# Output projection requests the attention's rows from its fifth chunk on, at its third chunk

## The chip, the cores and the metric

The kernel runs on one core of a Trainium2 chip. The metric is the device time of the program in microseconds (us), the median of several runs.

## The reference

One decoder block on 1024 tokens of width 1024, in f32. A joint projection `h @ w_in` feeds two groups of heads: an mLSTM (512 columns of output) and causal softmax attention with low-rank queries and keys (512 columns). Both outputs stand side by side and one output projection maps them back; then come a cross-attention into 256 memory tokens and a squared-ReLU MLP of hidden width 4096.

```python
y_m = jax.nn.sigmoid(o_pre) * hm.reshape(Bn, S, M_WIDTH)       # mLSTM group, 512 wide
...
o_a = causal_block_attention(q_full, k_full, v_a.transpose(0, 2, 1, 3))
y_a = rmsnorm(o_a.transpose(0, 2, 1, 3), a_out_g).reshape(Bn, S, A_WIDTH)
return jnp.concatenate([y_m, y_a], axis=-1) @ w_out
...
x = x + parallel_mixer(h, ...)
x = x + memory_cross_attention(rmsnorm(x, norm_x_g[l]), mem_n, ...)
x = x + jnp.square(jax.nn.relu(rmsnorm(x, norm_ffn_g[l]) @ w_ff1[l])) @ w_ff2[l]
```

So the first 512 of the 1024 inner columns of the product with `w_out` come from the mLSTM, the last 512 from the attention.

## The kernel before, in words

Every large product is cut into chunks of 128 inner columns. A chunk holds 12 matmuls of 128x512: 4 blocks of 128 outputs, each in three passes over high and low parts of the operands (`PASSES`). The parts are made by `split`: a cast on ACT (the high part) and a subtraction on DVE (the low part, the tiles `wu` and `yT`). Four PSUM banks with the tag `g` hold a group's sums.

The order of the work around the change comes from two things. `products(groups)` (L242) is a generator that walks the chunks of a list of groups: at each chunk it issues loads up to `ahead` = 3 chunks further on, splits one chunk further on, and then emits 4 blocks of matmuls, with `yield 0.65` after each. `Weaver.weave` (L152) takes these as fill: for each it lets attention tasks run for a share of its cost set by the group's `ratio`, chosen by priority and by modelled clocks. When the generator yields a list of names instead, `weave` calls `until`, which runs tasks and no fill at all until all those named are done. The order so written is then arranged again for each engine when the program is built; on the chip each engine takes its instructions in its own order.

The groups are, one after the other, the input projection of both token halves, the memory's keys and values, the output projection `w_out(0)` of tokens 0 to 511 (two groups of 512 outputs, 8 chunks each) and the query projection of the cross-attention for the same half (`q_group`, matmuls `g<-wu,x1s`). The attention tasks run beside `w_out(0)` and `q_group`: for each of 8 blocks of 128 queries two `mla_kv` (tiles `pk`, `ka`, `kT`), two `mla_q` (`pq`, `qa`, `rt`, `t`, `qT`), four `attn` (scores `pAS`, exponentials `P`, their transposes `pPT` copied to `PT`, sums `po`) and one `attn_fin` (L1080), which scales the rows `ya` by `as` (made on GpSimd) and writes them to `yd` in HBM (L1096). `w_out(1)`, for tokens 512 to 1023, comes when all attention tasks are done.

`w_out(h)` (L1099) reads back its rows from `yd`: chunk k loads `yr` (L1108) for four query blocks, from the mLSTM's half of `yd` for k = 0 to 3 and from the attention's half for k = 4 to 7. Four transposes (`pyT`), a cast and a subtraction make `yT`. Its first group names `need` = fin0 to fin3 (h = 0) or fin4 to fin7 (h = 1). In `products` this need does two things: loads ahead stop at the group's first chunk as long as one of those tasks is open, and at chunk 0 the list is yielded.

After the last attention task the program copies the query projection's sums to `xq` on DVE and ACT (with squares, `jkv` on DVE and `jk` on ACT, straight from the banks `g`), reads eight tiles `res` back, and transposes `xq` (`pxq`).

Of the kernel before, what the change touches and what calls it, by code (L numbers as in the profile page):

```python
# [19 lines left out]
NK = 8  # L20
# [15 lines left out]
class Engine:  # L36


    def __init__(self, eng, log, fixed, per):
        self.eng, self.log, self.fixed, self.per = eng, log, fixed, per  # L40
# [132 lines left out]
class Group:  # L173


    def __init__(self, w, c0, cols, act, evac, fm, nk=NK, gain=None, nblk=4, need=None, mkact=None, res=None, mark=None, pre=None, ratio=None):
        self.w, self.c0, self.cols, self.act, self.evac, self.fm = w, c0, cols, act, evac, fm
        self.nk, self.gain, self.nblk, self.need, self.mkact, self.res, self.mark, self.pre, self.ratio = (
            nk, gain, nblk, need, mkact, res, mark, pre, ratio)


class Trunk:
# [59 lines left out]
    def products(self, groups):  # L242

        T, ahead, near = self.T, self.ahead, self.near
        steps = [(g, k) for g in groups for k in range(g.nk)]
        loaded, units, ready = {}, {}, {}
        banks = [0.0] * 4
        nl = ns = 0
        ps = None
        for n, (g, k) in enumerate(steps):  # L250
            while nl < len(steps) and nl <= n + ahead:
                gg, kk = steps[nl]
                if gg.mkact is not None:
                    if gg.need is not None and nl > n:
                        if any(x not in self.wv.done for x in gg.need):
                            break
                    gg.mkact(kk, True)
                raw = self.raw([P, gg.cols])
                self.S.dma_start(raw, gg.w[kk * P:(kk + 1) * P, gg.c0:gg.c0 + gg.cols])
                loaded[nl] = raw  # L260
                nl += 1
            while ns < nl and ns <= n + near:
                gg, kk = steps[ns]
                if gg.mkact is not None:
                    gg.mkact(kk, False)
                u = self.wu([P, 2, gg.cols])
                self.split(u[:, 0], u[:, 1], loaded.pop(ns), None if gg.gain is None else self.vec(gg.gain, kk))
                ready[ns] = self.wv.settle(0.0)
                units[ns] = u
                ns += 1  # L270
            if k == 0:
                if g.mark is not None:
                    yield g.mark
                if g.ratio is not None:
                    yield (g.ratio,)
                if g.pre is not None:
                    yield from g.pre()
                if g.need is not None:
                    yield g.need
                ps = [self.pg.tile([P, HT], F32, tag="g", name="g") for _ in range(g.nblk)]  # L280
            u = units.pop(n)
            for j in range(g.nblk):
                for i, (x, y) in enumerate(PASSES):
                    st, sp = (k == 0 and i == 0), (k == g.nk - 1 and i == 2)
                    if g.fm:
                        T.matmul(ps[j], lhsT=u[:, x, j * P:(j + 1) * P], rhs=g.act[k][:, y, :], start=st, stop=sp)
                    else:
                        T.matmul(ps[j][:, :g.cols], lhsT=g.act[k][:, x, j * P:(j + 1) * P], rhs=u[:, y, :],
                                 start=st, stop=sp)
                self.wv.fready = 0.0  # L290
                if j == g.nblk - 1:
                    self.wv.fready = ready.get(n + 1, 0.0)
                elif k == 0:
                    self.wv.fready = banks[j + 1]
                yield 0.65
            if k == g.nk - 1:
                for j in range(g.nblk):
                    if g.res:
                        yield g.res
                    self.wv.settle(0.0)  # L300
                    g.evac(j, ps[j])
                    banks[j] = self.wv.settle(0.0)
                yield 0.0
# [141 lines left out]
    ratio = (1.416, 1.465, 1.465, 1.465, 1.465, 0.678, 1.0, 1.0, 0.5, 0.5, 1.186, 0.61, 0.915)  # L445
# [653 lines left out]
    def w_out(self, h):  # L1099

        V, S, T = self.V, self.S, self.T
        act, loc = [None] * NK, {}
        res = h == 1

        def mkact(k, load):
            if load:
                loc[k] = self.raw([P, 4, P], "yr")
                S.dma_start(loc[k], self.yd[4 * h:4 * h + 4, k // 4, :, (k % 4) * P:(k % 4 + 1) * P]  # L1108
                            .rearrange("b p d -> p b d"))
                return  # L1110
            ps = self.mp(name="pyT")
            for j in range(4):
                T.transpose(ps[:, j * P:(j + 1) * P], loc[k][:, j, :], self.ident)
            t = self.ap.tile([P, 2, HT], F32R, tag="act", name="yT")
            self.split(t[:, 0], t[:, 1], ps)
            act[k] = t

        def evac(g):
            def ev(j, ps):
                k = 4 * g + j  # L1120
                if k == 0:
                    loc["st"] = self.scr.tile([P, HT], F32, tag="st", name="st1", bufs=1)
                xr = self.raw([P, HT], "xres")
                S.dma_start(xr, self.a["xT"][k * P:(k + 1) * P, h * HT:(h + 1) * HT])
                if not res:
                    V.tensor_tensor(xr, ps, xr, ALU.add)
                    S.dma_start(self.x1d[k], xr)
                    self.stats_add(loc["st"], xr, k == 0)
                else:
                    V.tensor_tensor(self.R[h][k], ps, xr, ALU.add)  # L1130
                    self.stats_add(loc["st"], self.R[h][k], k == 0)
                if k == NK - 1:
                    self.stats_cols(loc["st"], self.v1[h], None)
            return ev

        need = [f"fin{4 * h + j}" for j in range(4)]
        w = self.a["w_out"]
        return [Group(w, 0, 512, act, evac(0), True, gain="gy", need=need, mkact=mkact),
                Group(w, 512, 512, act, evac(1), True, gain="gy")]


# [645 lines left out]
```

## Time and profile before

| what | value |
|---|---|
| runs | 1261.75, 1263.88, 1268.05 us; median 1263.88 |
| the profiled execution | 1264.9 us, span 1263.1 us |
| mean granted clock | 0.997 |
| PE busy | 1234.6 us, 98% of the span |
| DVE busy | 894.9 us, 71% |
| ACT busy | 662.0 us, 52% |
| GpSimd busy | 72.6 us, 6% |

Read it so: PE is what the kernel is made of, and 1 us less idle time on PE is at most 1 us less of the whole. The stretches that matter here are the attention's, from about 263 us to 464 us, and the passage to the cross-attention behind it, up to about 490 us. A row of a timeline gives the start, the duration, the engine, the line, the operation with its output and inputs, the number of alike instructions in a row, and in brackets the idle time before it with what ended it. Nearly all rows carry L56, the helper that records every operation, so the tile names are what to go by.

### The profile page before, as it was taken

How to read it: one execution, taken by the hardware profiler on the slowest of the kernel's cores; microseconds unless marked ns; L12 is line 12 of the kernel's file. 1: busy time of each engine (PE TensorE's matmuls, PEld its weight loads, DVE VectorE, ACT ScalarE, POOL GpSimd, SP SyncE). 2: the span in 40 equal slices, each digit the busy share in tenths (PEclk: the TensorE clock that was granted, in tenths of full speed). 3: DMA queues.
4: the chain of work that ended last, by engine and by line, in shares of the span. 5: the costliest groups of instructions: out<-in, count | busy, mean ns of one | idle time of the engine just before them, and what ended most of it. 6: DMA issues, size and time to landing. Idle time of an engine off the chain costs nothing.

```text
span 1263.1 us, 17573 instructions
## 1 busy us (share of the span) xinstructions
PE 1234.6 (98%) x6030; PEld 1011.2 (80%) x6030; DVE 894.9 (71%) x1919; ACT 662.0 (52%) x1536; POOL 72.6 (6%) x90
## 2 busy tenths in 40 slices
PE   7999999999999999999999999999999999999998
PEld 5777777777888887888777888888888888888887
DVE  5886897898757556757889976567657959654653
ACT  6466645688645446636655444454444444444442
POOL 1100100143200001001000000000000000000000
PEclk9999999999999999999999999999999999999999
DMA  7345533312124255332434654534399943333431
GB/s 242 89 117 176 161 99 109 117 60 92 51 92 126 87 179 178 99 126 100 167 101 133 210 190 167 184 136 147 117 334 314 319 149 101 100 100 100 155 129 66
DMA packets 113168, 180.65 MB, mean 143 GB/s; under 512 B 8472, under 2 KB 40120, under 8 KB 113080
## 3 DMA queue, kind: packets, MB, share of 16 engines
q1 hardware_dynamic: 113080, 179.55, 43.1%
q8 instruction: 47, 0.77, 0.3%
q14 instruction: 41, 0.34, 0.1%
HBM read 134.41 MB, written 45.11 MB: 142 GB/s over the span
## 4 chain that ended last, share of the span: by engine, by line
PE 81%; DVE 7%; DMA 4%; issue 4%; ACT 3%; POOL 1%; SPq 0%; POOLq 0%; DVEq 0%; ACTq 0%
PE gf L56 46%; PE g L56 21%; PE pAS L56 3%; PE po L56 2%; DMA xr<-in_xT_dram 1%; PE pPT L56 1%; DVE res L56 1%; PE pxo L56 1%; DMA xt<-in_x_dram 1%; DVE wu L56 1%; PE pq L56 1%; ACT wu L56 1%; PE pyT L56 1%; PE pxS L56 1%; PE qkps L56 1%
## 5 line engine op out<-in xcount | busy, mean ns | idle before, releaser
L56 PE MATMUL gf<-hu,w2u 128*128 128x512 f32 x1344 | 304.8, 389 | 0.0
L56 PEld LDWEIGHTS gf<-hu,w2u 128*128 128x128 f32 x1344 | 252.3, 188 | 52.4
L56 PE MATMUL gf<-xT,w1u 128*128 128x512 f32 x768 | 183.2, 397 | 2.1 <-ACT w1u L56 2.1
L56 PEld LDWEIGHTS gf<-xT,w1u 128*128 128x128 f32 x768 | 145.0, 189 | 37.9 <-ACT w1u L56 2.8
L56 ACT CAST hu<-hr 128x512 fp32r<-128x512 f32 x112 | 69.8, 624 | 169.7 <-PE gf L56 169.7
L56 PE MATMUL g<-wu,xs 128*128 128x512 f32 (+1 forms) x576 | 143.2, 399 | 10.1 <-ACT wu L56 7.5
L56 DVE TENSOR_TENSOR hu<-hr,hu 128x512 fp32r<-128x512 f32 x112 | 77.2, 689 | 100.9 <-ACT hu L56 100.9
L56 PEld LDWEIGHTS g<-wu,xs 128*128 128x128 f32 x576 | 106.6, 190 | 37.5 <-ACT wu L56 9.0
L56 PE MATMUL gf<-xB,w1u 128*128 128x512 f32 x576 | 135.1, 392 | 0.0
L56 PEld LDWEIGHTS gf<-xB,w1u 128*128 128x128 f32 x576 | 108.0, 188 | 24.4 <-issue 0.5
L56 ACT CAST w1u<-w1r 128x512 fp32r<-128x512 f32 x96 | 58.9, 619 | 116.1 <-PE gf L56 114.5
L56 DVE TENSOR_TENSOR wu<-raw,wu 128x512 fp32r<-128x512 f32 (+1 forms) x112 | 75.9, 678 | 48.4 <-ACT wu L56 48.0
L56 PE MATMUL g<-yT,wu 128*128 128x512 f32 x384 | 107.2, 410 | 1.4 <-ACT yT L56 1.4
L56 ACT CAST wu<-raw 128x512 fp32r<-128x512 f32 (+1 forms) x112 | 68.3, 613 | 67.5 <-PE g L56 49.3
L56 DVE TENSOR_TENSOR w1u<-w1r,w1u 128x512 fp32r<-128x512 f32 x96 | 65.8, 688 | 33.6 <-ACT w1u L56 33.4
L56 DVE TENSOR_TENSOR c<-gf,c 128x512 f32<-128x512 f32 x80 | 54.7, 688 | 40.0 <-PE gf L56 39.9
L56 PEld LDWEIGHTS g<-yT,wu 128*128 128x128 f32 x384 | 68.6, 192 | 13.3 <-ACT yT L56 1.9
L56 DVE TENSOR_TENSOR w2u<-w2r,w2u 128x512 fp32r<-128x512 f32 x112 | 76.7, 685 | 0.0
L56 ACT CAST w2u<-w2r 128x512 fp32r<-128x512 f32 x112 | 68.9, 615 | 4.4 <-PE gf L56 4.4
L56 ACT ACTIVATE c<-c 128x1024 f32<-128x1024 f32 x56 | 59.4, 1062 | 7.8 <-DVE c L56 5.4
L56 PE MATMUL g<-xs,wu 128*128 128x512 f32 x192 | 48.4, 401 | 0.4 <-ACT mraw L56 0.4
L56 PE MATMUL g<-oT,wu 128*128 128x512 f32 x192 | 47.6, 398 | 0.2
(428 smaller groups left out, 1862.2 us busy)
## 6 DMA issues: line engine op xcount, KB each, us to landing
hd<-c SPq DMA_DIRECT2D x56, 512.0 KB, 3.5
hr<-hd SPq DMA_DIRECT2D x56, 512.0 KB, 3.6
w1r<-in_w_dram SPq DMA_DIRECT2D x38, 512.0 KB, 3.9
w2r<-in_w_dram SPq DMA_DIRECT2D x32, 512.0 KB, 6.9
raw<-in_w_in_dram SPq DMA_DIRECT2D x48, 256.0 KB, 2.9
raw<-in_w_out_dram SPq DMA_DIRECT2D x32, 256.0 KB, 3.0
xr<-in_xT_dram SPq DMA_DIRECT2D x16, 256.0 KB, 3.6
xt<-in_x_dram SPq DMA_DIRECT2D x16, 256.0 KB, 3.4
```

What stands on the lines that cost most here:

```text
L56: return f(*args, **kw)
```

## The change

A group gets a number `from_k`, 0 unless given. The first group of `w_out` gets 4. Loads ahead then stop only at chunks from `from_k` on, and the list of needed tasks is yielded at chunk `from_k - 2` (the third) instead of chunk 0.

```diff
+    def __init__(self, ..., ratio=None, from_k=0):
...
+        self.from_k = from_k
...
         for n, (g, k) in enumerate(steps):
+            if g.need is not None and k == g.from_k - 2 >= 0:
+                yield g.need
             while nl < len(steps) and nl <= n + ahead:
                 gg, kk = steps[nl]
                 if gg.mkact is not None:
-                    if gg.need is not None and nl > n:
+                    if gg.need is not None and nl > n and kk >= gg.from_k:
                         if any(x not in self.wv.done for x in gg.need):
                             break
                     gg.mkact(kk, True)
...
-                if g.need is not None:
+                if g.need is not None and g.from_k == 0:
                     yield g.need
...
-        return [Group(w, 0, 512, act, evac(0), True, gain="gy", need=need, mkact=mkact),
+        return [Group(w, 0, 512, act, evac(0), True, gain="gy", need=need, mkact=mkact, from_k=4),
                 Group(w, 512, 512, act, evac(1), True, gain="gy")]
```

The first place is PE where the tasks up to fin3 run out. Before, the two products `pq` of a query block stood apart, each with other work behind it:

```order
L56 MATMUL pq<-wuq,cT 128x384 x6
L56 MATMUL pAS<-kT,qT 128x384 x3
L56 MATMUL pAS<-krz,qT 128x384 x2
...
L56 MATMUL pPT<-ident,P 128x128 x3
L56 MATMUL g<-yT,wu 128x512
L56 MATMUL pq<-wuq,cT 128x384 x6
L56 MATMUL po<-Va,PT 128x128 x7
L56 MATMUL pPT<-ident,P 128x128 x5
L56 MATMUL g<-yT,wu 128x512 x2
```

Now they stand back to back:

```order
L56 MATMUL g<-yT,wu 128x512 x2
L56 MATMUL pPT<-ident,P 128x128 x4
L56 MATMUL pq<-wuq,cT 128x384 x12
L56 MATMUL po<-Va,PT 128x128 x4
L56 MATMUL pAS<-kT,qT 128x384 x3
L56 MATMUL pAS<-krz,qT 128x384 x2
L56 MATMUL pAS<-kT,qT 128x256 x3
...
L56 MATMUL pkT<-ident,ka 128x128 x2
L56 MATMUL pPT<-ident,P 128x128 x3
L56 MATMUL g<-yT,wu 128x512
L56 MATMUL po<-Va,PT 128x128 x3
```

Between the second `pq` and the last `po` shown there are 22 other PE instructions (4 of `po`, 5 `pAS` of 384 columns, 5 of 256, the mask with its weights, 2 `pkT`, 3 `pPT`, 1 `g`), and the `po` behind them is the reader of the copy below. On DVE, both groups' normalisation and rotation now stand in one run ahead of the copy `PT<-pPT` that this last `po` reads:

```order
L56 SCALAR_TENSOR_TENSOR jkv,qm__4225<-qa 128x128
...
L56 SCALAR_TENSOR_TENSOR jkv,qm__4247<-qa 128x128
...
L56 TENSOR_TENSOR t_4292<-qa,rcos 128x128
L56 TENSOR_TENSOR rt<-qa,rsin 128x2x32 x2
L56 SCALAR_TENSOR_TENSOR kT<-pkT,kgain,kT 128x2x128
...
L56 TENSOR_TENSOR t_4312<-qa,rcos 128x128
L56 TENSOR_TENSOR rt<-qa,rsin 128x2x32 x2
L56 TENSOR_TENSOR anm<-anm 128x1
L56 COPY PT<-pPT 128x384
```

Thus 24 DVE rows of the two groups are ahead of a copy that PE waits for.

The second place is PE at the end of the attention and the passage to the cross-attention. Before, the query projection's last 48 matmuls came behind the last `po`:

```order
L56 MATMUL po<-Va,PT 128x128 x4
L56 MATMUL g<-wu,x1s 128x512 x48
L56 MATMUL pyT<-ident,yr 128x128 x4
L56 MATMUL g<-yT,wu 128x512 x4
L56 MATMUL pyT<-ident,yr 128x128 x4
L56 MATMUL g<-yT,wu 128x512 x8
L56 MATMUL pxq<-ident,xq 128x128 x8
```

Now the attention's last tasks outlast the query projection, and `pxq` stands right behind the last `po`:

```order
L56 MATMUL g<-wu,x1s 128x512 x18
L56 MATMUL pPT<-ident,P 128x128 x4
L56 MATMUL g<-wu,x1s 128x512 x3
L56 MATMUL po<-Va,PT 128x128 x4
L56 MATMUL pPT<-ident,P 128x128 x4
L56 MATMUL pyT<-ident,yr 128x128 x8
L56 MATMUL po<-Va,PT 128x128 x4
L56 MATMUL pxq<-ident,xq 128x128 x8
L56 MATMUL pyT<-ident,yr 128x128
L56 MATMUL g<-yT,wu 128x512 x12
```

On DVE, the copies of `xq` that `pxq` reads now stand behind the last block's chain:

```order
L56 COPY PT<-pPT 128x512 x2
L56 TENSOR_TENSOR yT<-pyT,yT 128x512 x2
L56 COPY ya<-po 128x128
L56 SCALAR_TENSOR_TENSOR jkv,ams<-ya 128x128
L56 TENSOR_SCALAR ams<-ams 128x4
L56 SCALAR_TENSOR_TENSOR ams<-als,ams 128x4
L56 TENSOR_TENSOR ya<-ya,as 128x512
L56 SCALAR_TENSOR_TENSOR wu<-raw,vecs,wu 128x512
L56 TENSOR_SCALAR xe_5726<-v_95 128x4
L56 COPY xq<-g 128x512 x2
```

So the last block's write-out is ahead of the copies on DVE, and no product of the query projection is left behind the last `po`. On SP the loads `yr` of `w_out(1)`'s chunks 0 to 3 now stand ahead of the last block's `yd` and of the eight reads `res`; before, all but the `yr` of chunk 0 stood behind them.

## Rows read from the trace of the kernel before

**Rows 1.** The page's first part: busy time and share of each engine
```profile
PE 1234.6 (98%) x6030; PEld 1011.2 (80%) x6030; DVE 894.9 (71%) x1919; ACT 662.0 (52%) x1536; POOL 72.6 (6%) x90
```
**Rows 2.** Busy time by stretch: PE, PEld, DVE, ACT, POOL, clock, DMA share, GB/s
```profile
305.00:325.00 20.00, 19.48 (x127) 16.30 (x125) 17.72 (x70) 15.69 (x55) 6.10 (x7) 1.00 0.16 60
325.00:350.00 25.00, 23.39 (x158) 20.45 (x156) 16.67 (x59) 13.34 (x51) 2.99 (x3) 1.00 0.17 54
...
400.00:463.00 63.00, 63.00 (x376) 53.57 (x374) 35.47 (x80) 30.06 (x74) 2.64 (x3) 1.00 0.35 109
...
480.00:482.00 2.00, 2.00 (x7) 1.62 (x6) 1.08 (x2) 1.70 (x3) 0.00 (x0) 0.50 0.69 206
```
**Rows 3.** Timeline of PE, the tasks up to fin3
```profile
314.88 0.94 PE L56 MATMUL g<-yT,wu 128*128 128x512 f32 x3
...
332.23 1.22 PE L56 MATMUL pq<-wuq,cT 128*128 128x384 f32 x6
333.28 1.72 PE L56 MATMUL po<-Va,PT 128*128 128x128 f32 x14
...
342.30 0.55 PE L56 MATMUL pPT<-ident,P 128*128 128x128 f32 x3 [1.37 <-ACT P L56]
```
**Rows 4.** Timeline of DVE: the steps of one query group, and a copy of transposes
```profile
334.27 0.28 DVE L56 SCALAR_TENSOR_TENSOR jkv<-qa 128x128 bf16<-128x128 f32 x1
...
334.94 0.36 DVE L56 TENSOR_SCALAR qm__4232<-qm__4232,evv 128x2 f32<-128x2 f32 x2
...
339.87 0.47 DVE L56 SCALAR_TENSOR_TENSOR qa<-qa,qs__4233,rowp 128x64 f32<-128x64 f32 x2
...
341.06 0.15 DVE L56 TENSOR_TENSOR anm<-anm 128x1 f32<-128x1 f32 x1
341.13 0.55 DVE L56 TENSOR_REDUCE anm<-pAS 128x1 f32<-128x384 f32 x1
...
342.89 0.56 DVE L56 COPY PT<-pPT 128x384 f32<-128x384 f32 x1 [0.35 <-PE pPT L56]
```
**Rows 5.** Timeline of SP: loads of chunks 0 and 3, writes of fin2 and fin3, chunk 4
```profile
262.36 0.38 SPq L1108 DMA_DIRECT2D yr<-yd  x1
...
296.73 0.37 SPq L1108 DMA_DIRECT2D yr<-yd  x1
...
322.86 17.14 SPq L1096 DMA_DIRECT2D yd<-ya  x2
341.79 0.37 SPq L1108 DMA_DIRECT2D yr<-yd  x1
```
**Rows 6.** Timeline of PE, from the last attention sums to the cross-attention
```profile
463.70 11.17 PE L56 MATMUL g<-wu,x1s 128*128 128x512 f32 x48
474.71 0.60 PE L56 MATMUL pyT<-ident,yr 128*128 128x128 f32 x4
476.47 1.43 PE L56 MATMUL g<-yT,wu 128*128 128x512 f32 x4 [1.17 <-ACT yT L56]
479.14 1.12 PE L56 MATMUL pyT<-ident,yr 128*128 128x128 f32 x4 [1.25 <-DMA yr<-yd]
479.91 3.30 PE L56 MATMUL g<-yT,wu 128*128 128x512 f32 x8
...
487.12 3.01 PE L56 MATMUL pxS<-kmT,xqT 128*128 128x256 f32 x24
489.97 1.55 PE L56 MATMUL g<-yT,wu 128*128 128x512 f32 x6
```
**Rows 7.** Timeline of DVE: the last block's chain and the copies of xq
```profile
464.39 0.28 DVE L56 COPY ya<-po 128x128 f32<-128x128 f32 x1
...
466.63 0.69 DVE L56 TENSOR_TENSOR ya<-ya,as 128x512 f32<-128x512 f32 x1 [1.21 <-POOL as L56]
467.45 0.69 DVE L56 TENSOR_TENSOR wu<-raw,wu 128x512 fp32r<-128x512 f32 x1
...
472.87 0.69 DVE L56 COPY xq<-g 128x512 f32<-128x512 f32 x1 [1.89 <-PE g L56]
```

More of the change, by code (lines that the diff above doesn't have):

```diff
@@ L173, with __init__ @@
 class Group:
-    def __init__(self, w, c0, cols, act, evac, fm, nk=NK, gain=None, nblk=4, need=None, mkact=None, res=None, mark=None, pre=None, ratio=None):
+    def __init__(self, w, c0, cols, act, evac, fm, nk=NK, gain=None, nblk=4, need=None, mkact=None, res=None, mark=None, pre=None, ratio=None, from_k=0):
         self.w, self.c0, self.cols, self.act, self.evac, self.fm = w, c0, cols, act, evac, fm
```

## The prediction

> **What bounds the kernel now.** I read the page's busy times first: PE is busy 98% of the span, DVE 71%, ACT 52% [rows 1]. So only idle time on PE can be won, 1263.1 - 1234.6 = 28.5 us in the whole span, and anything that makes PE wait is paid in full. The busy times by stretch come next, because the change touches only the attention's part and the passage behind it. PE is idle 0.52 us of 305 to 325, 1.61 us of 325 to 350, and not at all from 400 to 463 [rows 2]. So the request for fin0 to fin3, which falls before 340, costs at most about 2.1 us today. Then the timeline of PE: matmuls of `w_out(0)` already run at 314.88, far ahead of fin3 [rows 3], since the mLSTM's chunks 0 to 3 are loaded from 262.36 on [rows 5]; the build already moved chunk 0 up, whatever the request says. The last look is at the end of the attention: behind the last `po` stand 48 matmuls of the query projection, 11.0 us from start to start (0.229 each). During these DVE works off the last block: `ya` copied at 464.39, scaled at 466.63 after a wait of 1.21 on GpSimd, the next two steps done by 468.14 [rows 6, 7]. Only then come 1.17 us idle for `yT`, 1.25 us for `yr`, and a stretch at granted clock 0.50, the lower of the two levels (1.2 GHz) [rows 2, 6].
>
> **The change, part by part.** No operation is added or removed on PE; the matmuls, loads and splits of `w_out(0)` are the same. What moves is attention work against fill: up to 24 matmuls of chunks 0 and 1, 24 x 0.229 = 5.5 us of PE, are now spent as fill ahead of the request, and the attention's tasks come that much later against the products. Everything before 305 and from the late chunks of `w_out(1)` on keeps its order, so I cost it at nothing.
>
> First place, the request. Today the two `pq` of a block stand 5 us apart, with PE full between them. Now they are back to back, and DVE holds both groups' normalisation and rotation in one run ahead of the copy `PT` for which a `po` waits. I add up this run [rows 4]. Norms of one group: from 334.27 to the end of `qm` at 335.30, 1.0, and a third `jkv` 0.3, twice: 2.6. Rotation: 339.87 to 341.06, 1.2, twice: 2.4. Two reductions, up to 0.55 each: 1.0. A squared sum 0.3, the first group's last `t` 0.3, three tiny steps of 0.15, and `kT`, about as long as a copy, 0.4: together about 1.4. The copy itself 0.56. Sum about 7.9 us, counted from the end of the first `pq`. PE has meanwhile the second `pq` (1.05 from its start to the next [rows 3], so 0.175 for each matmul of 384 columns), four `po` and six other small ones at 0.12 (14 in 1.72 [rows 3]) 1.2, five `pAS` of 384 columns 0.9, five of 256 at 0.119 (24 `pxS` in 2.85 [rows 6]) 0.6, and one `g` 0.23: 4.0. So PE stands 3.9 us; if `qs` from GpSimd is waited for inside the run, as `as` was with 1.21 [rows 7], and the copy of `qa` delays its start by some 0.5, it is 5.6. I take 4.5.
>
> DVE takes the steps in their written order: at 466.63 it stood 1.21 us for GpSimd, and `wu`, which needs nothing of it, began only at 467.45 behind it [rows 7]. The Trainium skill, "Perfetto Trace Analysis", section "Tensor Engine Instruction (MATMUL, LD_WEIGHTS)", says that DVE, ACT and GpSimd are strict FIFO; the trace agrees with the 1.21 above.
>
> Behind this stall stand three smaller things. `pkT` needs `ka`, which DVE or ACT copies in the same press: 0 to 1.5, taken as 0.5. fin3's `ya` also comes behind the run, so its write and chunk 4's `yr` follow later; today 341.79 minus the second write's end at 340.0 is 1.8 [rows 5], and the load takes some us more, with `g` and `po` in front of it: 0 to 1.3, taken as 0.5. And the clock: after the two idles of 1.17 and 1.25 us eight matmuls took 3.30 instead of 8 x 0.229 = 1.83 [rows 6], 1.5 us lost; after a stall of 4.5 I take 1.2, between 0 and 1.5. Together 6.7 (3.9 to 9.9). From this goes the idle time that the same stretch has today, 2.1 [rows 2], most of it one wait of 1.37 [rows 3]: **+4.6** (+1.8 to +7.8).
>
> Second place, the passage. Today 474.71 to 489.97, 15.26 us, hold 12 `pyT` and 8 `pxq` (20 x 0.12 = 2.4), 24 `g` (5.5) and 24 `pxS` (2.85), together 10.75: 4.5 lost [rows 6]. Now the attention ends last, and the 11 us of products that covered its last block are gone: they run earlier, between attention tasks. Counted from the last `pPT`, PE has 8 `pyT` and 4 `po`, 12 x 0.12 = 1.4 us, before `pxq`. DVE must first copy `PT` (0.69, as a copy of 512 columns [rows 7]), do two subtractions of `yT` of 0.69 each, copy `ya`, and go through its chain [rows 7], 464.39 to 468.14, 3.75, before the copy of `xq`, 0.69: about 6.5 to 7.0. PE stands 5.1 to 5.6 where it was covered. Then the four banks `g` come free only as DVE and ACT read them for `xq` and its squares, so chunk 0 of `w_out(1)` is paced: 0 to 2.2, taken as 1.2; and the clock falls again, 0.5 to 1.5, taken as 1.0. Sum 7.5 (5.6 to 9.3) against 4.5: **+3.0** (+1.1 to +4.8). Already in it: the loads `yr` of chunks 0 to 3 now stand on SP ahead of the last `yd` and the eight `res`, so the wait of 1.25 for `yr` goes, and the stall for `xq` is late in its place.
>
> Between the two places attention is spread thinner among more products; PE was full there already (63.00 of 63.00 from 400 to 463 [rows 2]), so nothing can be won; some 0.5 us of small idles before 400 may go: -0.6. The sum is 4.6 + 3.0 - 0.6 = **+7.0 us**, +3 to +11. The profiled execution took 1264.9, so its like after the change would take 1271.9; the median of the runs is 1.0 lower, 1263.88, and I forecast 1263.88 + 7.0 = **1270.9 us** as median.
>
> **The rivals.** *The waits are hidden*: DVE is busy 16.67 of the 25 us around the request [rows 2], so it has slack, and the run could be started early enough; then the first place gains 1 to 2 us and the second loses as much: about 1264. Against it: the order is fixed and the 7.9 us of DVE work stand against 4.0 of PE.
>
> *Faster*: the extra 5.5 us of products ahead of the request cover the 2.1 us of idle around it, and the earlier `yr` takes the 4.5 us out of the passage with its half-rate stretch: 1263.88 - 6.6 = 1257.3. It decides itself at `xq`: if its banks are read before the last block's chain holds DVE, within the 1.4 us that PE has, nothing waits. For it: the wait of 1.25 on `yr` [rows 6] is one that an earlier load removes. Against it: the copy stands behind the chain. The Trainium skill, "DMA: Bandwidth & Descriptors", section "Rules for kernel authors", advises to issue a DMA early and wait on its semaphore late, which is what the change does; by that rule alone the time would be this rival's, and the trace bears it out only for that one wait.
>
> *It does nothing*: chunks 0 to 3 are loaded from 262 to 297 and chunk 0 is multiplied at 314.88 already [rows 3, 5], so the later request may only rename what the build did: 1263.9. Against it: the order does differ, from 305 to about 495.
>
> *A larger loss*: both stalls at their upper ends, and the clock down after each for longer than the eight matmuls seen: 7.8 + 4.8 + 2 = 14.6, 1278.5.
>
> **How the numbers follow.** A measurement of this kernel can tell about 0.5%, 6.3 us, from no change. The forecast has 0.62 chance, the hidden waits 0.14, faster 0.09, nothing 0.04, the larger loss 0.11. Of the forecast's +3 to +11 some six tenths lie above +6.3. Slower by over 0.5%: 0.38 + 0.11 = 0.49. Faster: a little over half of its rival, since -6.6 is at the edge: 0.05. Within: 0.24 + 0.14 + 0.04 + 0.04 = 0.46. The range leaves out most of the faster rival and the upper half of the larger loss: 1261.0 to 1278.0. The forecast's own range is 1267 to 1275.
>
> **What would show it.** After the change: a gap of 4 to 5 us on PE around 330 to 345, in front of a `po` and released by DVE's `PT`; a gap of about 5 us in front of `pxq` released by DVE's `xq`, with `ya<-ya,as` and `wu` just ahead of it there; a stretch near clock 0.5 after each; no wait for `yr` at chunk 1 of `w_out(1)`; the same time from the late chunks of `w_out(1)` to the end. I would be wrong if the gaps on PE from 300 to 490 together come out no longer than today's, or if the MLP's part shifts by more than 1 us.

## The result, and the profile after

The change makes the kernel slower: 1272.38 us median of six runs (1271.17 to 1274.03), against 1266.62 us of the kernel before on the same chips (1261.75 to 1268.05), ratio 1.0054, interval 1.0040 to 1.0068. The forecast was 1270.9 us, slower by 7.0; measured are 5.8 by the medians and 6.8 by the ratio on 1263.88. The profiled execution has a span of 1269.4 us, 6.3 more than before.

The page's first part, which answers to [rows 1]:

```profile
PE 1236.3 (97%) x6030; PEld 1013.8 (80%) x6030; DVE 896.0 (71%) x1925; ACT 660.1 (52%) x1530; POOL 73.2 (6%) x90
```

The work is the same, so the 6.3 us are time in which PE stands (1269.4 - 1236.3 = 33.1 us, before 28.5) or is longer busy with the same instructions (1.7 us more), which is the lower clock. From the `pq` at 302.50 (302.15 before) to the first matmul of the second half's query projection PE takes 552.50 - 302.50 = 250.0 us, before 545.56 - 302.15 = 243.4: +6.6, so all of the difference lies there. The first two rows are the starts after the change, the next two those of the kernel before (timelines of PE):

```profile
302.50 1.31 PE L56 MATMUL pq<-wuq,cT 128*128 128x384 f32 x6 [0.34 <-DVE kT L56]
...
552.50 7.22 PE L56 MATMUL g<-wu,x1s 128*128 128x512 f32 x31
```

```profile
302.15 1.31 PE L56 MATMUL pq<-wuq,cT 128*128 128x384 f32 x6 [0.34 <-DVE kT L56]
...
545.56 7.25 PE L56 MATMUL g<-wu,x1s 128*128 128x512 f32 x31
```

The view of waits of PE after the change, for 300 to 350 and then 350 to 500, names what stands there (total, times, longest):

```profile
PE po L56 <- DVE PT L56: 3.5, 1, 3.5
...
PE pxq L56 <- DVE xq L56: 4.8, 1, 4.8
PE pyT L56 <- ACT xP L56: 1.7, 1, 1.7
```

At the first place the timeline of PE, to be read against [rows 3], shows the two `pq` as one group, work until 340.9, and the stall in front of `po`; the windows behind it show the clock (columns as in [rows 2]):

```profile
335.31 2.36 PE L56 MATMUL pq<-wuq,cT 128*128 128x384 f32 x12
337.51 1.05 PE L56 MATMUL po<-Va,PT 128*128 128x128 f32 x8
...
344.39 1.65 PE L56 MATMUL po<-Va,PT 128*128 128x128 f32 x6 [3.50 <-DVE PT L56]
345.83 1.06 PE L56 MATMUL pyT<-ident,yr 128*128 128x128 f32 x4
346.68 1.12 PE L56 MATMUL pPT<-ident,P 128*128 128x128 f32 x5
347.56 0.72 PE L56 MATMUL g<-yT,wu 128*128 128x512 f32 x2
```

```profile
342.00:344.00 2.00, 0.00 (x0) 0.00 (x0) 2.00 (x11) 0.10 (x1) 1.33 (x1) 1.00 0.00 0
344.00:346.00 2.00, 1.61 (x7) 1.61 (x8) 1.22 (x3) 1.03 (x4) 0.66 (x1) 0.52 0.03 8
346.00:348.00 2.00, 2.00 (x12) 1.95 (x11) 0.46 (x1) 1.02 (x3) 0.00 (x0) 0.62 0.35 131
```

DVE is busy all of 342 to 344 while PE does nothing. Its timeline gives the run, of which [rows 4] showed the pieces: the first `jkv` at 337.40, after waiting for ACT's copy of `qa`, the two rotations, then the copy `PT`:

```profile
337.40 0.29 DVE L56 SCALAR_TENSOR_TENSOR jkv<-qa 128x128 bf16<-128x128 f32 x1 [2.05 <-ACT qa L56]
...
340.64 0.47 DVE L56 SCALAR_TENSOR_TENSOR qa<-qa,qs__4226,rowp 128x64 f32<-128x64 f32 x2
...
342.50 0.48 DVE L56 SCALAR_TENSOR_TENSOR qa<-qa,qs__4248,rowp 128x64 f32<-128x64 f32 x2
...
343.79 0.55 DVE L56 COPY PT<-pPT 128x384 f32<-128x384 f32 x1
```

At the second place, to be read against [rows 6, 7], PE has nothing between the last `po` and `pxq`, and DVE goes through the last block's chain before `xq`. The rows of PE first, then those of DVE:

```profile
477.82 1.16 PE L56 MATMUL po<-Va,PT 128*128 128x128 f32 x8
483.73 1.67 PE L56 MATMUL pxq<-ident,xq 128*128 128x128 f32 x8 [4.75 <-DVE xq L56]
485.19 0.42 PE L56 MATMUL pyT<-ident,yr 128*128 128x128 f32 x1
485.56 3.90 PE L56 MATMUL g<-yT,wu 128*128 128x512 f32 x12
...
498.03 0.66 PE L56 MATMUL pyT<-ident,yr 128*128 128x128 f32 x4 [1.69 <-ACT xP L56]
```

```profile
479.33 0.28 DVE L56 COPY ya<-po 128x128 f32<-128x128 f32 x1
...
481.56 0.69 DVE L56 TENSOR_TENSOR ya<-ya,as 128x512 f32<-128x512 f32 x1 [1.21 <-POOL as L56]
482.17 0.74 DVE L56 SCALAR_TENSOR_TENSOR wu<-raw,vecs,wu 128x512 fp32r<-128x512 f32 x1
...
482.90 1.28 DVE L56 COPY xq<-g 128x512 f32<-128x512 f32 x2
```

The wait of 1.69 for `xP` at 498.03 was in no part of the forecast. SP's timeline and the chain that ended last (last three rows) tell where it is from:

```profile
482.28 0.32 SPq L1100 DMA_DIRECT2D yd<-ya  x1
482.65 4.61 SPq L1170 DMA_DIRECT2D res<-x1d  x8
487.31 0.91 SPq L1178 DMA_DIRECT2D vmem<-vmd  x2
488.50 0.33 SPq L263 DMA_DIRECT2D raw<-in_w_out_dram  x1
...
488.50 5.38 DMA raw<-in_w_out_dram
...
494.66 0.76 DVE L56 SCALAR_TENSOR_TENSOR wu<-raw,vecs,wu 128x512 fp32r<-128x512 f32 x1 [3.52 <-ACT wu L56]
495.33 1.28 DVE L56 TENSOR_REDUCE xnm<-pxS 128x2 f32<-128x512 f32 x2
```

SP, too, takes its list in order: the last block's `yd` waits for `ya`, the eight `res` and two `vmem` go out behind it, and only then the weights of `w_out(1)`'s third chunk. They come 5.4 us later, DVE's `wu` waits for them, the maxima `xnm` stand behind `wu`, and `pyT` needs a bank that `xP` still reads.

### The profile page after: what moved, and what is told of

Read it like the earlier page. It is cut to its first block, busy times and chain, and to the rows that moved or that the text cites. A ratio compares the mean times of both kernels' runs of the same rounds, so it can differ in the third digit from the quotient of the medians.

```text
span 1269.4 us, 17562 instructions
## 1 busy us (share of the span) xinstructions
PE 1236.3 (97%) x6030; PEld 1013.8 (80%) x6030; DVE 896.0 (71%) x1925; ACT 660.1 (52%) x1530; POOL 73.2 (6%) x90
## 4 chain that ended last, share of the span: by engine, by line
PE 78%; DVE 8%; DMA 5%; issue 4%; ACT 4%; POOL 1%; SPq 0%; POOLq 0%; DVEq 0%; ACTq 0%
PE gf L56 45%; PE g L56 20%; PE pAS L56 2%; PE po L56 2%; DMA xr<-in_xT_dram 2%; DVE res L56 1%; PE pPT L56 1%; PE pxo L56 1%; DVE wu L56 1%; DMA xt<-in_x_dram 1%; PE pq L56 1%; DVE jkv L56 1%; DMA raw<-in_w_out_dram 1%; ACT wu L56 1%; PE pxS L56 1%
## 5 line engine op out<-in xcount | busy, mean ns | idle before, releaser
L56 PE MATMUL g<-wu,x1s 128*128 128x512 f32 x192 | 48.1, 398 | 0.0
```

Source lines behind the costliest of these rows:

```text
L56: return f(*args, **kw)
```

## The experiments

Each run is compared with the kernel before, run beside it. In this table the third column is the sum of PE's waits in the views of 300 to 360 and 360 to 510 of the profiled execution, the fourth the number of matmuls of the query projection behind the attention's last `po`.

| run | ratio to before (95%) | PE's waits, us | matmuls behind `po` | two `pq` in a row |
|---|---|---|---|---|
| before | 1 | 2.3 + 2.9 | 48 | no |
| the change | 1.0054 (1.0040 to 1.0068) | 4.0 + 6.8 | 0 | yes |
| load_only | 0.9990 (0.9975 to 1.0004) | 2.5 + 3.8 | 42 | no |
| req_only | 1.0001 (0.9989 to 1.0013) | 2.3 + 4.2 | 6 | no |
| q058 | 1.0024 (1.0011 to 1.0038) | 4.1 + 3.2 | 18 | yes |
| o089 | 0.9976 (0.9964 to 0.9987) | 1.0 + 3.0 | 48 | no |
| front_act | 1.0030 (1.0017 to 1.0043) | 3.1 + 6.8 | 0 | yes |
| xq_act | 1.0044 (1.0027 to 1.0060) | 4.6 + 7.0 | 0 | yes |
| before_o089 | 0.9987 (0.9972 to 1.0002) | 1.0 + 4.3 | 54 | no |
| o094 | 1.0014 (0.9998 to 1.0031) | 2.2 + 4.8 | 30 | no |
| res_late | 1.0045 (1.0029 to 1.0062) | 4.1 + 4.8 | 0 | yes |
| three_fixes | 1.0024 (1.0010 to 1.0039) | 2.9 + 4.1 | 0 | yes |
| o089_res_late | 0.9972 (0.9956 to 0.9987) | 1.0 + 3.0 | 48 | no |
| before_res_late | 0.9990 (0.9976 to 1.0003) | 2.3 + 2.5 | 48 | no |

The ratio goes with the sum of the waits: 4.0 us in the two fastest runs, 8.9 to 11.6 us in the four slowest.

**The halves of the change apart.** load_only lets the loads go ahead as in the change and puts the request back at chunk 0:

```diff
-            if g.need is not None and k == g.from_k - 2 >= 0:
+            if g.need is not None and k == 0 and g.from_k:
                 yield g.need
```

> The loads ahead of the change alone: chunks 0 to 3 may be loaded early, the request stays at chunk 0. In its order the two pq before fin3 stand apart and 42 matmuls of the query projection stand behind the attention's last po. Theory (two stalls made by DVE's order, of 3.5 us before a po and 4.75 us before pxq): neither stall, PE idle in the two places together at most 5 us as before, time within 2 us of before (ratio 0.998 to 1.002). Rival 1 (the earlier loads and their place among SP's and the DMA's other traffic cost the time): 4 to 6 us more than before, like the change.

The ratio is 0.9990, no loss, and neither stall is there. But SP's timeline of this run shows that the loads of the passage hardly moved: the `yr` of `w_out(1)`'s second chunk goes out behind the eight `res`, as before the change.

```profile
472.71 3.74 SPq L1170 DMA_DIRECT2D res<-x1d  x8
...
477.89 0.37 SPq L1112 DMA_DIRECT2D yr<-yd  x1
```

So the run shows that the permission to load ahead costs nothing by itself, and not yet that early loads (rival 1) cost nothing. req_only keeps the request at the third chunk and stops the loads as before:

```diff
-                    if gg.need is not None and nl > n and kk >= gg.from_k:
+                    if gg.need is not None and nl > n:
```

> The later request alone: yielded at the third chunk, loads ahead stop as before. In its order the two pq stand apart, and only 6 matmuls of the query projection (1.4 us) stand behind the last po. Theory: no stall before the po, a stall of 4.75 - 1.4, about 3.4 us, before pxq; 2 to 4 us more than before. Rival 2 (the later request costs by itself, because attention work is put off): 5 to 7 us more than before, spread or in both places.

The stall before `pxq` is there and shorter, 2.70 us where 3.4 were expected behind 6 matmuls, but the time is that of before, 1.0001, and my 2 to 4 us were wrong. The timeline of PE:

```profile
474.24 1.63 PE L56 MATMUL g<-wu,x1s 128*128 128x512 f32 x6
475.70 1.03 PE L56 MATMUL pyT<-ident,yr 128*128 128x128 f32 x8
479.44 1.94 PE L56 MATMUL pxq<-ident,xq 128*128 128x128 f32 x8 [2.70 <-DVE xq L56]
```

What I left out: a stall for `xq` takes the place of the two waits of before (1.17 for `yT`, 1.25 for `yr` [rows 6]), it does not come on top of them. This run also speaks against rival 1: three of the four `yr` that the change has on SP ahead of `res` stand there here, too, the third at 473.62 with `res` from 477.88 on, and no time is lost.

```profile
473.62 0.37 SPq L1112 DMA_DIRECT2D yr<-yd  x1
```

Neither half of the change makes the loss by itself.

**The same change with other orders.** q058 keeps the order of the changed kernel up to the query projection and gives the last group a smaller ratio, so that more attention work runs beside it:

```diff
-    ratio = (..., 0.5, 0.5, 1.186, 0.61, 0.915)
+    ratio = (..., 0.5, 0.5, 1.186, 0.61, 0.58)
```

> The changed kernel with the query projection's ratio at 0.58 instead of 0.915, so that more attention work runs beside it. The order up to the end of the output projection is that of the changed kernel (both pq in a row); 18 matmuls (4.1 us) stand behind the last po instead of none. Theory: the stall of 3.5 us before the po stays, the one before pxq falls from 4.75 to at most 1 us; some 4 us less than the changed kernel, 1 to 3 us more than before (ratio 1.001 to 1.0025). Rivals 1 and 2: the time of the changed kernel, ratio 1.005.

```profile
PE po L56 <- DVE PT L56: 3.6, 1, 3.6
...
PE pyT L56 <- DMA yr<-yd: 2.2, 1, 2.2
```

By its waits the first stall stays at 3.6 and that for `xq` is gone, with one of 2.2 for `yr` later in the passage; 0.3% of the 0.54% came back, and the ratio is that of the theory. o089 changes the ratio of the output projection's first group instead:

```diff
-    ratio = (..., 0.5, 0.5, 1.186, 0.61, 0.915)
+    ratio = (..., 0.5, 0.5, 0.89, 0.61, 0.915)
```

> The changed kernel with the ratio of the output projection's first group at 0.89 instead of 1.186: the request is still at the third chunk and the loads still go ahead, but in its order the two pq stand apart, and 48 matmuls stand behind the last po, as before the change. Theory: neither stall, time within 2 us of before, ratio 0.9985 to 1.0015. Rivals 1 and 2: ratio 1.004 to 1.006, since loads and request are those of the change.

With the change's rules for loads and request, 0.9976: not only is the loss gone, it is faster than before by more than the interval, and faster than the 0.9985 that I expected at best. Of PE's waits from 300 to 360 only 1.0 us is left (2.3 before). So the loss belongs to the order that the change got with its ratio of 1.186, and not to the later request in every order. o094, the same with 0.94, shows how narrow this is:

> The changed kernel with that ratio at 0.94: the two pq apart, 30 matmuls (6.9 us) behind the last po, eight transposes of y together ahead of pxq. Theory: no stall before a po above 1.5 us; the chain to xq takes some 6 us after the last po, covered by 6.9 us; ratio 0.997 to 1.000. Rivals 1 and 2 (loads, request): 1.004 to 1.006.

```profile
483.10 0.71 PE L56 MATMUL pxq<-ident,xq 128*128 128x128 f32 x5
...
490.22 0.50 PE L56 MATMUL g<-yT,wu 128*128 128x512 f32 x1 [2.87 <-ACT wu L56]
```

The theory had `pxq` right, which waits for nothing behind 30 matmuls, and the time not: PE stands 2.87 for the weights of the second chunk instead. before_o089 asks what of the gain is the ratio's:

> The kernel before with the ratio of the output projection's first group at 0.89, request and loads untouched. The run with the change and this ratio took 0.9976 of before. Theory that this gain needs the change (chunks 0 to 1 as fill ahead of the request, with the wait of 1.37 us at 342.30 gone): here that wait stays, the passage has 54 matmuls behind the last po, ratio 0.999 to 1.001. Rival (the gain is the ratio's alone): ratio 0.9965 to 0.9985.

0.9987 lies between the two expectations, and its interval overlaps that of o089. The wait of 1.37 for `P` [rows 3], which I expected to stay, is down to 0.3 here as well; in the passage PE waits 3.2 for `yr`, where o089 waits 1.2. Whether the gain of o089 needs the change is not settled.

**The queue itself.** front_act leaves all as in the changed kernel and has one copy made by ACT, the `PT` for which PE waited (the planner's clocks are charged as before):

```diff
-            self.copy(PT[:, :n], pt[:, :n])
+            if (blk, i, c) == (4, 0, 0):
+                self.log.append((V.eng, V.fixed + n * V.per))
+                self.nc.scalar.copy(PT[:, :n], pt[:, :n])
+            else:
+                self.copy(PT[:, :n], pt[:, :n])
```

> The changed kernel with the one copy of 384 transposed columns on which PE waited 3.5 us made by ACT instead of DVE; PE's order is that of the changed kernel up to that place. Theory (DVE's queue made the wait): the wait of 3.5 us for this copy falls below 1 us. Next late are the exponentials behind it, since their maxima still stand at the end of DVE's run: a new wait of 1 to 2 us before the following five transposes of P. Net 1 to 2.5 us less than the changed kernel, ratio to before 1.003 to 1.0045. Rival (PE waits there for something else, the copy's input or the load): the wait stays above 3 us.

```profile
341.46 0.94 PE L56 MATMUL po<-Va,PT 128*128 128x128 f32 x6 [0.37 <-ACT PT L1072]
342.63 0.66 PE L56 MATMUL pyT<-ident,yr 128*128 128x128 f32 x4 [0.23 <-DVE kT L56]
343.96 1.20 PE L56 MATMUL g<-yT,wu 128*128 128x512 f32 x4 [0.68 <-ACT yT L56]
...
350.63 0.66 PE L56 MATMUL pyT<-ident,yr 128*128 128x128 f32 x4 [1.09 <-DMA yr<-yd]
```

3.50 became 0.37, and the granted clock stays at 1.00 from 340 to 352: DVE's queue made the stall. The ratio is 1.0030, as expected, the intervals of the two runs just overlap. Some 2.2 of the 3.1 us came back as other waits (4.0 to 3.1 in the table): `yT`, and 1.09 for chunk 4's `yr`, because fin3's `ya` still stands at the end of DVE's run. The exponentials that I expected next cost PE nothing, since four `g` stand ahead of `pPT` there.

xq_act does the same with the first copy of `xq`:

```diff
-        self.copy(qs, pv)
+        if b in (0,):
+            self.log.append((self.V.eng, self.V.fixed + 512 * self.V.per))
+            self.nc.scalar.copy(qs, pv)
+        else:
+            self.copy(qs, pv)
```

> The changed kernel with the first copy of xq made by ACT instead of DVE; what stands ahead on PE is the same. Theory: the copy no longer stands behind the last block's chain on DVE, only behind ACT's wu, which ended at 481.1 in the changed kernel; the wait before pxq falls from 4.75 to about 2.7 us. The banks are still read late, so 1 to 2 us less than the changed kernel, ratio to before 1.0035 to 1.0045. Rival (pxq is late because the attention as a whole ends late): the wait stays above 4 us.

```profile
481.67 1.29 PE L56 MATMUL pxq<-ident,xq 128*128 128x128 f32 x7 [2.66 <-ACT xq L1270]
...
498.93 1.11 PE L56 MATMUL pyT<-ident,yr 128*128 128x128 f32 x4 [3.78 <-ACT xP L56]
```

The wait falls to 2.66, and the bank of `xP` takes all of it back, 1.69 to 3.78. So the second place has two limits one behind the other, and the first was not the last. res_late tests the second, with the eight reads of `res` issued with the last loads of `w_out(1)`:

```diff
-        for k in range(NK):
-            S.dma_start(self.R[0][k], self.x1d[k])
...
+        def mkact(k, load):
+            mk(k, load)
+            if load and k == NK - 1:
+                for i in range(NK):
+                    S.dma_start(self.R[0][i], self.x1d[i])
...
+        wout[0].mkact = mkact
```

> The changed kernel with the eight reads of res issued among the output projection's last loads instead of ahead of its third: the load raw of the third chunk then stands on SP right behind the last yd. Theory (the wait of 1.69 us for the bank of xP at 498 comes from that load, issued at 488.50 behind res and vmem): it falls below 0.7 us, the 4.75 us before pxq stay; 1 to 2.5 us less than the changed kernel, ratio to before 1.003 to 1.0045. Rival (the bank is late because of DVE's queue): the wait of 1.7 us stays.

```profile
484.67 0.32 SPq L1100 DMA_DIRECT2D yd<-ya  x1
485.33 0.33 SPq L263 DMA_DIRECT2D raw<-in_w_out_dram  x1
```

The load now goes out right behind `yd`, and the wait for `xP` is gone from PE's waits, where 4.8 for `xq` alone is left from 360 to 510: SP's queue made it. The time hardly shows it (1.0045, at the edge of what was expected, and not to be told from the change's 1.0054): in this execution the clock stayed low for longer behind the stall, 12 `g` taking 4.65 us instead of 3.90. three_fixes puts all three together:

> The changed kernel with the three things together: the copy of 384 columns and the first copy of xq on ACT, and res late. Theory: with the wait for res out of the way, the 2 us won before pxq are no longer given back (in the run with the copy of xq alone the wait for xP's bank rose from 1.69 to 3.78); waits at pxq near 2.7 us, at the bank below 1.5 us; ratio to before 0.999 to 1.002. Rival (the change's loss lies in the order as a whole): 1.003 and more.

1.0024, a little more than half of the loss gone, between what I and the rival expected: `pxq` still waits 3.0 for ACT's `xq`, the bank of `xP` 1.1, and the small waits around the request add up to 2.9. I put the rest down to the missing cover; no run isolates it. Last, res late with the faster order and with the kernel before:

> The fastest version so far (the change with the ratio 0.89, 0.9976 of before) with res late as well. There 1.20 us of PE are lost for yr, issued behind res, 1.17 for yT and about 1.5 at the lower clock. Theory: the wait for yr goes, with it most of the stretch at the lower clock; 1.5 to 3.5 us less, ratio to before 0.995 to 0.9965. Rival (the passage is bounded by yT and the banks): no gain, 0.997 to 0.998.

> The kernel before with res late alone. Theory: the waits of 1.25 us for yr and part of the 1.17 us for yT and of the lower clock behind them go: 1.5 to 3.5 us less, ratio 0.997 to 0.999. It tells what of the last run's gain needs the change. Rival: no gain, 0.9995 to 1.0005.

Neither gives a gain that can be told: 0.9972 beside 0.9976, where I had expected 0.9965 or less, and 0.9990 with an interval across 1. The wait for `yr` is gone in both, and `pxq` waits for `xq` instead, 1.62 us in the first:

```profile
476.25 0.33 PE L56 MATMUL pxq<-ident,xq 128*128 128x128 f32 x1 [1.62 <-ACT xq L56]
477.74 0.50 PE L56 MATMUL g<-yT,wu 128*128 128x512 f32 x1 [1.16 <-ACT yT L56]
```

The faster versions are o089 and o089_res_late, both ahead of the two kernels of this case.

## Why the prediction was right

The time, the side and the two places were right, and both stalls are released by the instruction that was named: `PT` on DVE in front of a `po`, and `xq` on DVE behind `ya<-ya,as` and `wu`. The runs that took the one copy off DVE (3.50 to 0.37, 4.75 to 2.66) show that the queue made each. The terms came out so:

- First place, forecast +4.6. The stall took 3.50, below my 3.9 to 5.6. DVE's part came out as summed: from the end of the first `pq` (336.5, an estimate: half of the row of 12 at 335.31) to the end of the copy `PT` are 7.8 us against 7.9, of them 0.9 until ACT's copy of `qa` is there and 6.9 of run (337.40 to 344.3). PE's 4.0 were too few: the four `po` that I took from the order are eight matmuls in the trace (row at 337.51), as seven of the order are 14 in [rows 3], which is 0.5 us more at 0.12 each. `pkT` and chunk 4's `yr`, 0.5 each, cost nothing. The clock cost about 1.4 as forecast (1.2): 15 small instructions from 344.39 to 347.56 took 3.17 instead of 15 x 0.12 = 1.8. With the 2.1 of before taken off, +2.8; the term was 1.8 too large.
- Second place, forecast +3.0. The stall took 4.75 (5.1 to 5.6; here, too, four `po` of the order are eight matmuls, 477.82, so it should have been 4.6 to 5.1), the pacing by the banks (1.2) is not to be seen, the clock cost 1.5 (1.0): 12 `g` in 3.74 us from start to start instead of 2.75, and 8 `pxq` in 1.46 instead of 0.96. What came unforeseen is the 1.69 for `xP`, SP's queue; I had the `yr` on SP in mind, and not that the third chunk's weights stand behind `res`. Sum 7.9 against 4.5 of before, +3.4; the term was nearly right by errors against each other, which is luck.
- Together 6.2, measured 6.6 between the two landmarks. The gain of 0.6 from small idles did not come.

One row was misread: `wu` at 467.45 [rows 7] was not held up by `ya`, since ACT's own part of `wu` (466.79, 0.62 long) ended only at 467.41. That DVE keeps its order is shown after the change: ACT's part is done at 481.12 (480.40 and 0.72), and DVE's `wu` starts at 482.17, behind the `ya` that waited for GpSimd.

Of the rivals, the faster one, that earlier loads take out the wait for `yr`, is right for that wait: after the change none is left in the passage. It goes with the place of `yr` on SP and not with the rule of the loads: load_only and o089 have this rule, their `yr` stands behind `res`, and they wait 0.77 and 1.20; req_only has not, its `yr` stands ahead, and no such wait is in its view. In its place stood the stall for `xq`, as the forecast said. The Trainium skill, "DMA: Bandwidth & Descriptors", section "Rules for kernel authors", advises to issue a DMA early and wait late. In the trace after the change that holds for this one wait, 1.25 before and none after, and does not decide the time. "The waits are hidden" falls with the 3.50 and 4.75, and "it does nothing" with the order that moved.

What the prediction did not see is that the loss is not the request's own. With the request moved alone it is 1.0001, and with the same change and another ratio 0.9976. The step "the attention's tasks come that much later" was right; that the planner's ratio can take it back was not considered.

## What to carry to other kernels

Where a planner fills PE from two streams, read what stands behind the last task of each: work that covers a chain on other engines is worth up to the length of the chain (18 matmuls, 4.1 us, took out the stall of 4.75 in q058), and a change that uses it earlier must leave some. Here one of the ratios that share the streams had to move with the request, and 0.94 instead of 0.89 already lost the gain. And when a stall has been taken out by moving one instruction, look for the queue of the same chain on the next engine (here SP behind DVE) before counting the gain.

## What the runs showed of the hardware

The clock did not follow the length of the idle stretches alone. Before the change two idles of 1.17 and 1.25 us had 0.50 behind them [rows 2, 6], and in before_res_late so had 1.03 and 1.16. In o089 the same place had idles of 1.17 and 1.20, and in o089_res_late 1.62 and 1.16, and the granted clock stayed at 1.00 in both. The windows of o089:

```profile
472.00:474.00 2.00, 0.83 (x4) 0.30 (x2) 1.93 (x13) 1.97 (x10) 1.48 (x2) 1.00 1.07 362
474.00:476.00 2.00, 0.81 (x3) 0.37 (x2) 1.03 (x7) 0.37 (x2) 1.52 (x2) 1.00 1.10 338
476.00:478.00 2.00, 1.99 (x11) 1.74 (x12) 0.68 (x2) 1.21 (x2) 0.00 (x0) 1.00 0.84 237
```

So a drop of the clock behind idles of this size is worth some 1.5 us when it comes, and one profiled execution does not tell whether it comes in the others. Executions of one kernel do differ in this: the mean granted clock of o089's twelve runs goes from 1.000 (1259.68 us) to 0.994 (1267.65 us), that of the 34 runs of the kernel before beside it from 1.000 (1261.74 us) to 0.993 (1271.01 us). The six runs of the change lie at 0.991 to 0.996, the profiled one at 0.996, so the clock may have more of the loss than the two profiles show (2.9 us against 1.5 before); how much is open.
